# The last step of blockwise triangular inverses as products of quarters, in a two-layer hybrid decoder trunk

## The chip, the cores and the metric

The kernel runs on one NeuronCore of a Trainium2 chip. The metric is device time in microseconds (us) from start to end of one execution, as a median over several runs. In the profile, PE is TensorE (PEld its weight loads), DVE is VectorE, ACT is ScalarE, POOL is GpSimd, and SP is SyncE, whose queue issues most DMAs.

## What is computed

One inference step of a decoder trunk with two layers, for 512 prompt positions and for 8 samples of 4 positions. In each layer an input projection feeds four mixers (RWKV-7, S5, gated delta, windowed attention), whose outputs are joined, projected and followed by an MLP. The change concerns RWKV-7 and gated delta alone. The gated delta mixer works on chunks of 64 positions and solves one lower triangular system for each chunk and head:

```python
def step(S, inp):
    qc, kc, vc, bc, gc = inp
    ...
    A = jnp.where(strict, bc[..., :, None] * decay * jnp.einsum('bhtd,bhjd->bhtj', kc, kc), 0.0)
    gam = jnp.exp(G)[..., None]
    rhs = bc[..., None] * (vc - gam * jnp.einsum('bhvk,bhtk->bhtv', S, kc))
    U = lax.linalg.triangular_solve(eye + A, rhs, left_side=True, lower=True, unit_diagonal=True)
    ...
```

RWKV-7 is a recurrence over single positions in the reference. The kernel puts it into the same form with chunks of 64. For both mixers the kernel computes the inverses of the unit triangular matrices themselves, 64x64 each, and multiplies with them.

## The kernel before

The prompt is cut in two halves of 256 columns, and the second half also carries the 32 sample columns. For each layer and half the kernel runs an input projection, the mixers, an output projection and an MLP. The projections and MLPs are the dense work: weights arrive by DMA as 128x512 parts (`wraw`), ScalarE casts each part to a high part `whi` (three buffers), VectorE subtracts to get the rest `wlo`, and TensorE makes 12 matmuls from each part (`dense`, `load_part`). The mixers of one half are interleaved with the dense work of another. The framework orders the instructions on each engine when the program is built, from modelled times and from the priorities in `PRIO`; on the chip each engine then runs its own list in that order.

A half has 4 chunks and 4 heads for each of the two mixers, so 16 triangular matrices of 64x64. They lie in a tile of 128 partitions x 8 x 64: chunks in the upper and the lower 64 partitions, 8 matrices side by side in each. `tri_begin` inverts the diagonal blocks of 16 on VectorE. `tri_end` then doubles the block size twice, from 16 to 32 and from 32 to 64. It holds `lt` (the strict triangle, transposed), `t16` (the inverse so far) and `t16t` (its transpose), and `work`. Its helper `mm` makes 16 matmuls with 64 rows, 64 columns of weights and 64 moving columns, two for each of the 8 places, on the two diagonal quarters of TensorE's array. The first doubling makes `lt * t16`, masks it (constant `blk16`, which is -1 in the blocks that are wanted and 0 elsewhere), and makes two products that are added to `t16` and `t16t`. The second doubling, the step that is changed, makes `lt * t16`, masks it with `blk32`, makes one more product with `t16t`, and adds it to `t16t`.

`rw_stage3` and `gd_stage3` call `tri_end`, and hand its result to `inv_apply`, which multiplies it with keys and values. With two layers, two halves and two mixers there are 8 calls. All matmuls are recorded under L220 (`mm` of the class), all `tt` operations on VectorE under L236, `acopy` under L232 (without scale) and L233 (with one). In the trace `t16`, `t16t`, `work` and RWKV's `lt` appear as `t`, and gated delta's `lt` as `g`.

Of the kernel before, what the change touches and what calls it, by code (L numbers as in the profile page):

```python
# [12 lines left out]
ALU = mybir.AluOpType  # L13
# [126 lines left out]
class K:  # L140
# [180 lines left out]
    def tri_end(self, lt, t16, t16t, work):  # L321
        def mm(a, b):

            out = self.ps([128, 8, 64])
            for hb in range(8):
                for c in range(2):
                    cs = slice(64 * c, 64 * c + 64)
                    self.mm(out[cs, hb], a[cs, hb], b[cs, hb])
            return out

        bm = lambda n: self.c(n).unsqueeze(1).to_broadcast([128, 8, 64])

        self.tt(work, mm(lt, t16), bm("blk16"))
        a, b = mm(t16t, work), mm(work, t16t)
        self.tt(t16, a, t16, ALU.add)
        self.tt(t16t, b, t16t, ALU.add)
        self.tt(work, mm(lt, t16), bm("blk32"))
        self.tt(t16t, mm(work, t16t), t16t, ALU.add)
        return t16t


# [1719 lines left out]
```

## Time and profile before

| | |
|---|---|
| median of 3 runs | 1626.77 us (1626.5 to 1631.62) |
| the profiled execution, whole | 1630.86 us |
| its span, first to last instruction | 1629.1 us |
| TensorE busy | 1555.1 us, 95% |
| VectorE busy | 1195.3 us, 73% |
| ScalarE busy | 961.8 us, 59% |
| GpSimd busy | 318.0 us, 20% |
| mean granted TensorE clock | 0.984 |

An fp32 matmul appears as two instructions, each with a weight load and a matmul. Durations of single matmuls overlap, since they are pipelined; the time that a group really takes is read from its starts. The busy time of a group is the union of its instructions' times.

### The profile page before, as it was taken

How to read it: one execution, taken by the hardware profiler on the slowest of the kernel's cores; microseconds unless marked ns; L12 is line 12 of the kernel's file. 1: busy time of each engine (PE TensorE's matmuls, PEld its weight loads, DVE VectorE, ACT ScalarE, POOL GpSimd, SP SyncE). 2: the span in 40 equal slices, each digit the busy share in tenths (PEclk: the TensorE clock that was granted, in tenths of full speed). 3: DMA queues.
4: the chain of work that ended last, by engine and by line, in shares of the span. 5: the costliest groups of instructions: out<-in, count | busy, mean ns of one | idle time of the engine just before them, and what ended most of it. 6: DMA issues, size and time to landing. Idle time of an engine off the chain costs nothing. (4 is left out here: it accounts for less than half of the span.)

```text
span 1629.1 us, 38773 instructions
## 1 busy us (share of the span) xinstructions
PE 1555.1 (95%) x14528; PEld 1453.4 (89%) x14528; DVE 1195.3 (73%) x2843; ACT 961.8 (59%) x2086; POOL 318.0 (20%) x618
## 2 busy tenths in 40 slices
PE   7989989899999999899999999999999999999996
PEld 7978978689889999888989999989888889999996
DVE  6898786976876867787595567879679755856665
ACT  6766648643455567765454467886444556755544
POOL 4751251000310428100020002620013001200001
PEclk9999999999999999999999999999999999999998
DMA  7645444443566565535365555535436655655552
GB/s 232 200 114 136 143 134 148 109 130 114 173 211 201 171 204 204 182 112 139 105 217 173 167 161 197 180 109 151 138 121 208 205 193 185 210 189 166 163 170 101
DMA packets 203112, 267.38 MB, mean 164 GB/s; under 512 B 81114, under 2 KB 95772, under 8 KB 202508
## 3 DMA queue, kind: packets, MB, share of 16 engines
q1 hardware_dynamic: 199180, 249.94, 48.9%
q0 software_dynamic: 3744, 14.96, 2.5%
q8 instruction: 114, 1.87, 0.5%
q14 instruction: 74, 0.61, 0.1%
HBM read 237.95 MB, written 28.58 MB: 164 GB/s over the span
## 5 line engine op out<-in xcount | busy, mean ns | idle before, releaser
L232 ACT CAST whi<-wraw 128x512 fp32r<-128x512 f32 x752 | 462.6, 619 | 419.2 <-PE ps L220 264.7
L236 DVE TENSOR_TENSOR wlo<-wraw,whi 128x512 fp32r<-128x512 f32 x752 | 534.9, 716 | 209.2 <-ACT whi L232 188.0
L220 PE MATMUL ps<-h,whi 128*128 128x288 f32 (+1 forms) x3264 | 519.5, 297 | 8.4 <-ACT h L228 4.4
L220 PEld LDWEIGHTS ps<-h,whi 128*128 128x128 f32 x3264 | 451.3, 191 | 25.8 <-ACT h L228 6.0
L220 PE MATMUL ps<-f,whi 128*128 128x288 f32 (+1 forms) x2752 | 421.9, 292 | 5.9 <-ACT whi L232 5.8
L220 PEld LDWEIGHTS ps<-f,whi 128*128 128x128 f32 x2752 | 372.0, 189 | 17.1 <-ACT whi L232 7.4
L220 PE MATMUL ps<-h,wlo 128*128 128x288 f32 (+1 forms) x1632 | 285.9, 295 | 5.4 <-DVE wlo L236 5.1
L220 PEld LDWEIGHTS ps<-h,wlo 128*128 128x128 f32 x1632 | 235.8, 191 | 12.3 <-DVE wlo L236 7.8
L220 PE MATMUL ps<-f,wlo 128*128 128x288 f32 (+1 forms) x1376 | 235.8, 292 | 1.7 <-DVE wlo L236 1.7
L220 PEld LDWEIGHTS ps<-f,wlo 128*128 128x128 f32 x1376 | 195.9, 189 | 5.3 <-DVE wlo L236 2.9
L236 POOL TENSOR_TENSOR sums<-sums,d 128x288 f32<-128x288 f32 (+1 forms) x54 | 51.2, 948 | 519.0 <-ACT d L228 517.7
L220 PE MATMUL ps<-r,r 64*64 64x64 f32 (+7 forms) x1184 | 67.8, 236 | 12.7 <-POOL r L236 3.8
L236 DVE TENSOR_TENSOR acc<-acc,ps 128x256 f32<-128x256 f32 (+1 forms) x96 | 41.7, 435 | 49.8 <-PE ps L220 49.7
L220 PEld LDWEIGHTS ps<-r,r 64*64 64x64 f32 (+4 forms) x1184 | 55.9, 140 | 23.2 <-issue 5.9
L232 ACT CAST f<-d 128x288 fp32r<-128x288 f32 (+1 forms) x128 | 53.3, 417 | 35.3 <-DVE d L236 35.3
L228 ACT ACTIVATE d<-ps 128x288 f32<-128x288 f32 (+1 forms) x152 | 59.8, 393 | 8.1 <-PE ps L220 6.1
L236 DVE TENSOR_TENSOR f<-d,f 128x288 fp32r<-128x288 f32 (+1 forms) x128 | 56.7, 443 | 7.4 <-ACT f L232 7.4
L236 DVE TENSOR_TENSOR d<-d 128x288 f32<-128x288 f32 (+1 forms) x128 | 56.7, 443 | 0.0
L228 ACT ACT_TABLE_LOAD x43 | 55.2, 1283 | 0.8
L220 PEld LDWEIGHTS ps<-t,t 64*64 64x64 f32 x1024 | 32.5, 135 | 4.7 <-issue 1.1
L220 PE MATMUL ps<-t,t 64*64 64x64 f32 x1024 | 36.3, 220 | 0.3 <-DMA t<-diag 0.2
L232 ACT COPY r<-ps 64x128 f32<-64x128 f32 (+2 forms) x56 | 20.4, 369 | 26.4 <-PE ps L625 11.6
(404 smaller groups left out, 1851.6 us busy)
## 6 DMA issues: line engine op xcount, KB each, us to landing
wraw<-in_w_up SPq DMA_DIRECT2D x256, 256.0 KB, 2.8
wraw<-in_w_down SPq DMA_DIRECT2D x256, 256.0 KB, 2.9
wraw<-in_w_in SPq DMA_DIRECT2D x176, 256.0 KB, 3.0
wraw<-in_w_out SPq DMA_DIRECT2D x64, 256.0 KB, 3.2
t<-diag SPq DMA_DIRECT2D x32, 128.0 KB, 3.2
x<-acc POOLq DMA_DIRECT2D x3, 1152.0 KB, 6.8
x<-acc POOLq DMA_DIRECT2D x3, 1024.0 KB, 6.4
xs<-mix SPq DMA_DIRECT2D x8, 288.0 KB, 2.9
```

The costliest lines, as they stand in the source:

```text
L220: return self.nc.tensor.matmul(out=out, lhsT=lhsT, rhs=rhs, start=start, stop=stop)
L228: return self.nc.scalar.activation(out=out, in_=in_, func=func, scale=scale, bias=bias, **kw)
L232: return self.nc.scalar.copy(out, in_)
L236: return (eng or self.nc.vector).tensor_tensor(out=out, in0=a, in1=b, op=op)
```

## The change

The second doubling no longer multiplies whole 64x64 blocks. Only the quarter that is wanted is computed: a product of 32x32 blocks, 16 of them for each product as before, with 32 rows, 32 columns of weights and 32 moving columns. The tile positions in the array change with it: rows 0 and 64 with columns 32 and 96 in the first product, rows 32 and 96 with columns 0 and 64 in the second. The mask with `blk32` on VectorE is gone. In its place ScalarE copies the first product from PSUM into `work` with the scale -1, in two operations on 32 partitions x 256 elements. The last addition on VectorE, before one operation on 128 partitions x 512 elements, becomes two on 32 partitions x 256 elements, which write only the quarter that changes.

```diff
         a, b = mm(t16t, work), mm(work, t16t)
         self.tt(t16, a, t16, ALU.add)
         self.tt(t16t, b, t16t, ALU.add)
-        self.tt(work, mm(lt, t16), bm("blk32"))
-        self.tt(t16t, mm(work, t16t), t16t, ALU.add)
+
+        def quarter(a, b, o):
+            out = self.ps([128, 8, 64])
+            for hb in range(8):
+                for c in (0, 64):
+                    k = slice(c + 32 - o, c + 64 - o)
+                    m = slice(o, o + 32)
+                    n = slice(32 - o, 64 - o)
+                    self.mm(out[c + o:c + o + 32, hb, 0:32], a[k, hb, m], b[k, hb, n])
+            return out[:, :, 0:32]
+
+        p = quarter(lt, t16, 32)
+        for c in (32, 96):
+            self.acopy(work[c:c + 32, :, 0:32], p[c:c + 32], scale=-1.0)
+        p = quarter(work, t16t, 0)
+        for c in (0, 64):
+            t = t16t[c:c + 32, :, 32:64]
+            self.tt(t, p[c:c + 32], t, ALU.add)
         return t16t
```

## Rows read from the trace of the kernel before

**Rows 1.** The page, part 1: busy us of each engine (share) xinstructions.
```profile
PE 1555.1 (95%) x14528; PEld 1453.4 (89%) x14528; DVE 1195.3 (73%) x2843; ACT 961.8 (59%) x2086; POOL 318.0 (20%) x618
```
**Rows 2.** Windows: length, then PE, PEld, DVE, ACT, POOL busy (instructions), PEclk, DMA.
```profile
133.00:190.00 57.00, 56.88 (x834) 51.54 (x833) 42.58 (x126) 32.45 (x95) 12.52 (x42) 1.00 0.50 150
327.00:377.00 50.00, 49.84 (x736) 44.16 (x735) 35.15 (x93) 23.92 (x59) 0.00 (x0) 1.00 0.44 124
745.00:795.00 50.00, 50.00 (x722) 44.80 (x721) 31.91 (x84) 21.68 (x53) 0.25 (x2) 1.00 0.40 118
1146.00:1189.00 43.00, 43.00 (x693) 38.75 (x691) 27.47 (x73) 18.63 (x46) 0.00 (x0) 1.00 0.41 120
sum 200.00, PE 199.72 PEld 179.25 DVE 137.10 ACT 96.69 POOL 12.77; mean PE 49.93 PEld 44.81 DVE 34.28 ACT 24.17 POOL 3.19
```
**Rows 3.** The chain that ended last, pieces: start us, us, what.
```profile
1167.60 27.17 PE ps L220 x446
```
**Rows 4.** Timeline of VectorE and TensorE: start us, us, instructions (merged).
```profile
147.96 0.67 DVE L236 TENSOR_TENSOR t<-ps,cst 128x512 f32<-128x512 f32 x1
149.97 1.15 PE L220 MATMUL ps<-t,t 64*64 64x64 f32 x32
```
**Rows 5.** Timeline of TensorE, 177 to 184 us.
```profile
177.32 1.15 PE L220 MATMUL ps<-t,t 64*64 64x64 f32 x32
178.40 0.45 PE L220 MATMUL ps<-r,r 128*64 128x64 f32 x8
...
183.04 0.27 PE L220 MATMUL ps<-rwS,r 64*64 64x64 f32 x1
...
183.26 0.44 PE L220 MATMUL ps<-rwS,r 64*64 64x64 f32 x5
```
**Rows 6.** Windows as in rows 2; the counts include matmuls still in flight.
```profile
154.90:154.96 0.06, 0.06 (x10) 0.06 (x9) 0.06 (x1) 0.00 (x0) 0.00 (x0) 1.00 0.89 205
154.90:155.08 0.18, 0.18 (x19) 0.18 (x16) 0.18 (x2) 0.00 (x0) 0.00 (x0) 1.00 0.86 196
141.80:141.90 0.10, 0.10 (x5) 0.10 (x6) 0.10 (x1) 0.04 (x1) 0.10 (x1) 1.00 0.96 328
141.80:143.07 1.27, 1.27 (x45) 1.27 (x46) 1.20 (x3) 0.04 (x1) 0.42 (x1) 1.00 0.51 152
```
**Rows 7.** Groups by form (rows*columns loaded, moving): xcount, busy us, mean ns, idle before.
```profile
L220 PE MATMUL ps<-t,t 64*64 64x64 f32 x1024 | 36.3, 220 | 0.3 <-DMA t<-diag 0.2
L220 PE MATMUL ps<-cv 64*64 64x128 f32 x96 | 5.1, 282 | 0.4 <-DVE g L236 0.4
L220 PE MATMUL ps<-c,s 64*64 64x8 f32 x128 | 4.6, 199 | 0.0
L220 PEld LDWEIGHTS ps<-t,t 64*64 64x64 f32 x1024 | 32.5, 135 | 4.7 <-issue 1.1 <-DMA t<-diag 1.0 <-DVE swst L236 0.2
L220 PEld LDWEIGHTS ps<-r,r 64*128 64x128 f32 x128 | 11.7, 187 | 4.2 <-DVE r L236 2.4 <-issue 1.0 <-DVE wlo L236 0.2
L220 PEld LDWEIGHTS ps<-cst,c 16*32 16x32 f32 x4 | 0.3, 102 | 0.0
```
**Rows 8.** VectorE groups by form; then L233 on ScalarE: ns min/median/max.
```profile
L236 DVE TENSOR_TENSOR t<-ps,t 128x512 f32<-128x512 f32 x24 | 16.4, 684 | 7.1 <-PE ps L220 7.1
L236 DVE TENSOR_TENSOR c<-ps,cst 32x256 f32<-32x256 f32 x16 | 5.6, 403 | 0.0
L233 ACT ACTIVATE g<-ps x8: 362/384/384, 160.1 to 1167.6; 128x256 f32<-128x256 f32 x8
```
**Rows 9.** Waits of ScalarE: who for whom, us in total, times, longest.
```profile
ACT whi L232 <- PE ps L220: 264.7, 285, 5.4
```
**Rows 10.** Timeline of ScalarE and TensorE near 234.4 us; a window after it.
```profile
238.61 0.63 ACT L228 ACTIVATE r<-r 128x512 f32<-128x512 f32 x1 [4.06 <-DVE r L245]
239.58 1.33 PE L220 MATMUL ps<-e,cst 128*128 128x288 f32 x2 [5.15 <-ACT e L232]
236.10:242.90 6.80, 3.32 (x12) 3.03 (x13) 4.13 (x11) 2.86 (x5) 5.84 (x18) 0.50 0.16 56
```

## The prediction

> **What bounds the kernel now.** I read the profile from the whole to the place of the change. The busy shares come first: TensorE is busy 95% of the span, VectorE 73%, ScalarE 59% [rows 1]. An average hides stages, so next come the busy times of the four stretches in which the eight inverses end (two in each, one for RWKV and one for gated delta): in 200 us TensorE is busy 199.72 us, VectorE 137.10, ScalarE 96.69, and the granted clock is 1.00 in all four [rows 2]. The chain of waits says the same from the other side: in these stretches it runs along TensorE itself, in the last of them for 27.17 us in one piece [rows 3]. So in these places the end is set by how long TensorE needs for its queue; a VectorE or ScalarE operation there costs nothing as long as its result is there before TensorE reaches the product that reads it.
>
> How much room that leaves: the mask step of the last 32-to-64 stage of one call starts at 147.96 us and takes 0.67 us; TensorE begins the product that reads it at 149.97 us, 1.34 us after its end [rows 4]. Of the sixteen VectorE results of this stage (eight masks, eight additions) this one has the least room. Dense matmuls fill the time between.
>
> **What one product costs.** A product is sixteen 64x64x64 matmuls, which stand in the trace as 32 instructions (fp32 is run as two). One such product starts at 177.32 us and the next work at 178.40 us: 1.08 us [rows 5]. In the steady state forty starts lie in the 1.17 us from 141.90 to 143.07 us (45 counted against 5), 29.3 ns each [rows 6]. Two diagonal quarters of the array work side by side, so one quarter takes about 58 ns for an instruction, and 32 x 29.3 = 0.94 us; the other 0.14 us is the first load and the change of tile shape.
>
> What sets these 58 ns? The form with 8 moving columns instead of 64 has 4.6 us for 128 instructions, 36 ns each, and the one with 64 columns 36.3 us for 1024, 35 ns [rows 7]. So fewer moving columns alone buy nothing. But that form still loads 64 columns of weights. Weight loads last 102 ns for 32 columns, 135 for 64, 187 for 128 [rows 7]: 0.8 to 1.0 ns a column, and 64 columns make some 53 ns. Matmuls go from 220 to 282 ns for 64 more moving columns [rows 7], 1.0 ns a column. Load and stream each need about 53 ns of the 58 and overlap; the rest, about 5 ns, is overhead. The change halves both sides, the loaded and the moving columns. I therefore take 27 + 5 = 32 ns for one quarter and 16 ns for an instruction with two quarters side by side.
>
> **The change, part by part.**
> *Products.* Sixteen products (two in each of eight calls) keep their 32 instructions and go from 29.3 to about 16 ns: 512 x 13.3 ns = 6.8 us less TensorE time. Bounds: nothing, if something other than the columns sets the pace; and 29.3 - 13 = 16 ns, 8.3 us, if the closest packing that the trace shows is reached: nine starts in 0.12 us, 13 ns each, where two groups of 64x64 matmuls overlap (19 counted against 10) [rows 6]. I take 6.8, nearest to the rows on columns, and hold the rate for possible because of that burst. No change of tile shape is added: a product stood between dense 128x128 work before and still does.
>
> *VectorE.* Removed: eight masks and eight additions over 128x512, 0.684 us each by the row of the additions, whose shape the masks have too [rows 8], 10.9 us. Added: sixteen additions over 32x256, 0.403 us by the row of that form [rows 8], 6.4 us. VectorE has 4.5 us less, hidden either way: it is idle for 63 of the 200 us [rows 2].
>
> *ScalarE.* Added: sixteen copies of 32x256 from PSUM with a constant scale; the nearest row, the same kind over 128x256, has 0.384 us [rows 8]: 6.1 us, hidden by the 103 us in which ScalarE is idle there. Thirty-two partitions could take half of it, and the stride in PSUM could double it, 3 to 12 us in all; either is far below that cover. If the cover were gone, all 6.1 us would stand on the path.
>
> *The chain of one call.* Before: product 1.08, mask 0.68, product 1.08, addition 0.68, 3.52 us. After: 0.65, two copies 0.77, 0.65, two additions 0.81, 2.88 us, where 0.65 is 32 x 16 ns and the same 0.14. It gets shorter, so the later reader has, if anything, more room than the 1.34 us above. The new wait is on ScalarE's queue: the copy waits there for its product, and behind it stand the casts of the dense weights, for which TensorE waits in turn. But those casts run ahead: ScalarE spends 264.7 us of the whole run waiting for TensorE to free a cast buffer [rows 9]. No DMA is moved, and SyncE's and GpSimd's queues get nothing new.
>
> **The sum.** The profiled execution took 1630.86 us, 1.8 us more than its span; 1630.86 - 6.8 = 1624.1 us. It lies 4.1 us above the median of the three runs, 1626.77 us, and the measured time will be a median: 1626.8 - 6.8 = 1620.0. I give 0.5 us back for the ends of the stretches, where TensorE waits on other engines: **1620.5 us**. What is late next after a stretch are waits on chains of GpSimd, VectorE and ScalarE; a stretch that ends 0.9 to 1.7 us earlier could lengthen them, but they hang on TensorE's products and move with it.
>
> **The rivals.** *First, the columns do not set the pace.* For it speaks that 8 and 64 moving columns go at the same 36 and 35 ns [rows 7]. If a floor on an instruction stands at the 24 ns that nine starts in the 0.22 us from 183.04 to 183.26 us show [rows 5], the gain is 512 x 5.3 ns = 2.7 us, 1624.1; if the pace is all floor, 1626.8. I put this rival at 1625. Against it speaks the burst of 13 ns. The Trainium skill, "TensorE: Matmul & The Clock Gate", section "Wait — 56ns, not 53.3ns?", states such a floor: start to start never below about 25 ns however few columns. By that figure, an estimate, the gain would be 512 x 4.3 = 2.2 us. This trace disagrees for instructions in different quarters, which start 13 ns apart, and cannot say whether it holds within one quarter of 32x32, where my 32 ns lies above it anyway.
>
> *Second, slower: ScalarE's queue holds TensorE up.* The order of instructions on each engine is fixed at build from modelled times, so new operations on two queues redraw it from the first inverse (133 us) to the end. The place where this costs is visible before: at 234.4 us TensorE stands still for 5.15 us because ScalarE's copy of a dense product is queued behind an S5 activation that itself waits 4.06 us for VectorE [rows 10]; and a stretch of 6.8 us at a granted clock of 0.50 (1.2 GHz) follows [rows 10], which costs up to 3.4 us more. One such event is 8.5 us. The sixteen copies wait in the same queue. The rival decides from the point where a copy waits longer than the 1.34 us and the casts ahead allow; 0.9 us of standstill in each of the eight calls eats the gain. Two new events of the full price give 1620 + 17 = 1637. Against it: in the four stretches before, TensorE lost only 0.28 us in all, with 46 to 95 ScalarE operations in each [rows 2].
>
> *Third, the redraw goes the other way* and removes that one event: 1620 - 8.5 = 1611.5. *Fourth, the gain is taken back in part* by the waits behind the stretches: 1624.
>
> **How the numbers follow.** About 0.3% (4.9 us) is what a measurement of this kernel can tell from no change. Forecast, 1617 to 1621.8: 0.45, counted as faster. Third rival, 1608 to 1616: 0.07, faster. First rival, 1623 to 1627: 0.19, same. Fourth, 1622 to 1626: 0.09, same. Slower rival, 1632 to 1642: 0.20. That makes 0.52 faster, 0.28 same, 0.20 slower. The forecast's own range is 1617 to 1622; to leave out no more than 2 in 10, the range reaches to 1612 below and to 1635 above, into the near half of the slower rival.
>
> **What would show it.** The 32x32 products in the profile of the changed kernel: 32 instructions from start to next start in about 0.65 us, 16 ns apart in the steady state, shows the first step right; 0.8 us or more, the first rival. Weight loads of 32x32 at about 102 ns show the halved load. ScalarE copies near 0.38 us and VectorE additions near 0.40 us, with TensorE busy throughout the four stretches, show the cover. TensorE's idle total and the stretches of granted clock 0.50 tell the second and third rival. The prediction is wrong if TensorE waits for the copies, or if its waits elsewhere move by more than the 6.8 us.

## The result and the profile after

The changed kernel takes 1641.11 us (median of 11 runs, 1636.13 to 1647.87), the kernel before 1631.62 us beside it (11 runs, 1626.50 to 1637.62). The ratio is 1.0062, 95% interval 1.0041 to 1.0083: 0.6% slower, clear of the noise, where 1620.5 us and 0.4% faster were forecast, and outside the range. The profiled execution took 1645.58 us with a span of 1643.8 us.

The local steps came out as worked out. First the page, part 1, of the changed kernel (to be held against rows 1):

```profile
PE 1568.3 (95%) x14528; PEld 1460.8 (89%) x14528; DVE 1195.3 (73%) x2843; ACT 966.7 (59%) x2102; POOL 316.2 (19%) x618
```

The windows of the four stretches in which its inverses end (rows 2; length, then PE, PEld, DVE, ACT, POOL busy, PEclk, DMA):

```profile
134.50:188.00 53.50, 53.36 (x754) 48.27 (x754) 41.38 (x121) 34.17 (x100) 12.79 (x44) 1.00 0.51 149
339.00:388.00 49.00, 49.00 (x712) 43.21 (x712) 33.46 (x89) 24.73 (x62) 0.00 (x0) 1.00 0.39 112
758.00:808.00 50.00, 50.00 (x746) 44.06 (x745) 30.47 (x82) 23.08 (x57) 0.65 (x2) 1.00 0.38 115
1157.00:1199.00 42.00, 42.00 (x682) 37.44 (x681) 25.47 (x66) 19.48 (x49) 0.00 (x0) 1.00 0.40 117
sum 194.50, PE 194.36 PEld 172.98 DVE 130.77 ACT 101.45 POOL 13.45; mean PE 48.59 PEld 43.24 DVE 32.69 ACT 25.36 POOL 3.36
```

The timeline of the first call's last step (rows 4 and 5), with lines in between left out:

```profile
146.04 0.69 PE L220 MATMUL ps<-t,t 32*32 32x32 f32 x32
...
146.66 1.34 PE L220 MATMUL ps<-h,whi 128*128 128x288 f32 x8
146.78 0.78 ACT L233 ACTIVATE t<-ps 32x256 f32<-32x256 f32 x2 [3.74 <-PE ps L220]
...
149.92 0.69 PE L220 MATMUL ps<-t,t 32*32 32x32 f32 x32
...
150.88 0.86 DVE L236 TENSOR_TENSOR t<-ps,t 32x256 f32<-32x256 f32 x2
```

And the groups by form (rows 7 and 8):

```profile
L220 PE MATMUL ps<-t,t 32*32 32x32 f32 x384 | 9.3, 193 | 0.0
L220 PEld LDWEIGHTS ps<-t,t 32*32 32x32 f32 x384 | 7.5, 107 | 2.3 <-issue 0.7 <-ACT xs L228 0.2
L236 DVE TENSOR_TENSOR t<-ps,t 32x256 f32<-32x256 f32 x16 | 6.6, 416 | 5.4 <-PE ps L220 5.1
L233 ACT ACTIVATE t<-ps 32x256 f32<-32x256 f32 x16 | 6.0, 376 | 5.7 <-PE ps L220 5.0 <-issue 0.2
```

A product of quarters takes 0.62 us from its first start (146.04) to the next work (146.66), where 1.08 us stood before. The copies end at 147.56 us, 2.36 us before TensorE reads them; in all eight calls they are done at least 1.9 us ahead. In the four stretches TensorE is busy for 194.36 of 194.50 us at the full clock, as before. So nothing at the place of the change explains a slower kernel.

The profiled spans do. Here is the mean granted clock, the changed kernel's first and the one of the kernel before under it:

```profile
core 0: 1643.8 us, clock 0.975
```

```profile
core 0: 1629.1 us, clock 0.984
```

At two levels, 1.00 and 0.50, that is 2 x 0.025 x 1643.8 = 82 us at half clock, against 2 x 0.016 x 1629.1 = 52 us; and the 30 us more of half clock are 15 us. By the pages TensorE is without work for 75.5 us of the span (1643.8 - 1568.3) against 74.0, so hardly any of the loss is a new wait. Where much of the additional half clock lies, four pairs of windows of the changed kernel show, each with the stretch ahead of a fall and the one behind it:

```profile
387.20:394.80 7.60, 7.60 (x187) 6.71 (x185) 3.54 (x21) 1.17 (x2) 1.07 (x2) 1.00 0.35 115
394.80:401.60 6.80, 6.80 (x29) 4.83 (x27) 3.01 (x13) 0.99 (x2) 0.00 (x0) 0.50 0.00 1
1238.10:1241.30 3.20, 3.20 (x59) 3.07 (x58) 2.01 (x6) 1.31 (x3) 0.50 (x2) 0.99 0.22 82
1241.30:1248.10 6.80, 6.80 (x45) 5.21 (x43) 2.88 (x8) 0.99 (x3) 0.37 (x2) 0.50 0.01 2
299.60:306.00 6.40, 3.75 (x37) 3.14 (x36) 6.30 (x23) 3.43 (x9) 0.00 (x0) 1.00 0.19 53
306.00:312.80 6.80, 4.39 (x27) 3.33 (x28) 6.45 (x13) 3.15 (x7) 0.59 (x1) 0.50 0.17 31
251.40:258.20 6.80, 4.96 (x28) 4.01 (x26) 4.47 (x11) 5.52 (x15) 0.00 (x0) 1.00 0.39 123
258.20:265.00 6.80, 6.34 (x26) 5.62 (x27) 2.37 (x8) 2.17 (x6) 0.00 (x0) 0.50 0.37 120
```

The first two pairs are the surprise: TensorE is busy for the whole of 7.60 us and of 3.20 us, and then the clock stands at 0.50 for 6.80 us. What it was busy with, its timeline in the changed kernel tells:

```profile
386.70 0.64 PE L220 MATMUL ps<-f,whi 128*128 128x256 f32 x4
387.27 1.15 PE L220 MATMUL ps<-g,t 64*64 64x64 f32 x32
...
393.65 1.22 PE L220 MATMUL ps<-c,s 64*64 64x8 f32 x35
394.80 2.07 PE L220 MATMUL ps<-r,cst 128*128 128x512 f32 x2
396.80 0.47 PE L220 MATMUL ps<-gdS,g 64*64 64x64 f32 x2
397.20 0.79 PE L220 MATMUL ps<-f,whi 128*128 128x256 f32 x2
```

Between the dense matmuls (`whi`, `wlo`) at 386.70 and at 397.20 us lie about 10 us; up to 394.80 us there are only matmuls on 64x64 and 128x64 parts of the array. The kernel before has work of the same kind there, and its dense matmuls come back after 5.6 us, at 387.6 us:

```profile
382.00:387.60 5.60, 5.60 (x154) 5.13 (x152) 3.15 (x20) 0.98 (x2) 1.07 (x2) 1.00 0.56 202
387.60:394.40 6.80, 6.80 (x56) 5.76 (x57) 5.21 (x24) 2.50 (x5) 0.00 (x0) 1.00 0.15 45
```

The second pair is of the same kind. In the changed kernel two groups that use little of the array stand back to back:

```profile
1238.19 1.97 PE L220 MATMUL ps<-cst,gdlb 32*128 32x32 f32 x16
1240.08 1.99 PE L220 MATMUL ps<-cv,s 64*64 64x8 f32 x50
```

In the kernel before their starts are 7.4 us apart, with dense matmuls between:

```profile
1223.45 1.97 PE L220 MATMUL ps<-cst,gdlb 32*128 32x32 f32 x16
...
1227.95 1.10 PE L220 MATMUL ps<-h,whi 128*128 128x256 f32 x8
...
1230.89 2.04 PE L220 MATMUL ps<-cv,s 64*64 64x8 f32 x64
```

The Trainium skill, "TensorE: Matmul & The Clock Gate", section "HAM oscillation — how this bites in real kernels", puts such falls down to gaps in which TensorE is idle. By that rule alone the falls at 394.8 and 1241.3 us would not be there; here the trace disagrees. It agrees for the third pair, where TensorE stands still for 3.33 us, waiting for VectorE:

```profile
308.06 0.44 PE L224 MATMUL ps<-cst,xs 128*128 128x128 f32 x1 [3.33 <-DVE r L236]
```

Ahead of the fourth fall TensorE is without work for 1.84 of 6.80 us, and 1.35 of them it waits for a cast of weights that stands behind other work in ScalarE's queue:

```profile
257.40 0.51 PE L220 MATMUL ps<-h,whi 128*128 128x256 f32 x2 [1.35 <-ACT whi L232]
```

That these two waits bring on the falls behind them was not tried; it needs another order on VectorE and ScalarE too.

None of these places holds an instruction that the change touches. But the framework drew the order anew at build: from the first inverse on, 3797 of the 11906 places in TensorE's list hold another instruction than before, 973 of 2809 in VectorE's, 469 of 2009 in ScalarE's and 139 of 997 in SyncE's, which issues the DMAs. So there were two theories to tell apart: *order* (the new list costs, the new work gains) and *work* (the quarters or the copies cost).

### The profile page after: what moved, and what is told of

It is laid out like the page before. It is cut to its first block, busy times and chain, and to the rows that moved or that the text cites. A ratio compares the mean times of both kernels' runs of the same rounds, so it can differ in the third digit from the quotient of the medians.

```text
span 1643.8 us, 38794 instructions
## 1 busy us (share of the span) xinstructions
PE 1568.3 (95%) x14528; PEld 1460.8 (89%) x14528; DVE 1195.3 (73%) x2843; ACT 966.7 (59%) x2102; POOL 316.2 (19%) x618
## 5 line engine op out<-in xcount | busy, mean ns | idle before, releaser
L220 PE MATMUL ps<-h,whi 128*128 128x288 f32 (+1 forms) x3264 | 524.8, 299 | 12.5 <-ACT h L228 5.9
L220 PEld LDWEIGHTS ps<-h,whi 128*128 128x128 f32 x3264 | 455.9, 193 | 31.2 <-ACT h L228 7.1
L220 PEld LDWEIGHTS ps<-h,wlo 128*128 128x128 f32 x1632 | 237.4, 192 | 13.5 <-DVE wlo L236 8.0
L220 PEld LDWEIGHTS ps<-t,t 64*64 64x64 f32 (+1 forms) x1024 | 27.8, 124 | 6.3 <-DMA t<-diag 2.0
L220 PE MATMUL ps<-t,t 64*64 64x64 f32 (+1 forms) x1024 | 31.8, 210 | 1.6 <-DMA t<-diag 1.5
```

The lines of the kernel that those rows point to most:

```text
L220: return self.nc.tensor.matmul(out=out, lhsT=lhsT, rhs=rhs, start=start, stop=stop)
```

## The experiments

**One word on the sums.** For each kernel the time lost to the clock is taken as (1 - mean granted clock) x span, averaged over its runs, and the rest is its mean time less that. A half-clock stretch in which TensorE idles anyway is counted too, and the rest scatters by some 3 us from run to run, so differences of it are good to 1 or 2 us at best. Within one kernel a us more of this loss went with only 0.56 us more time from run to run (199 runs), so the column says too much rather than too little; a count that doesn't rest on it stands behind e12. The changes of tile are counted in the trace: how often a TensorE matmul has another size of tile than the one before.

| kernel (runs) | ratio to before | mean us | lost to the clock | rest | changes of tile |
|---|---|---|---|---|---|
| before (23) | 1 | 1632.4 | 28.0 | 1604.3 | 536 |
| changed (11) | 1.0062 [1.0041, 1.0083] | 1642.1 | 38.8 | 1603.3 | 574 |
| e1 new work, old order (12) | 0.9972 [0.9958, 0.9986] | 1627.6 | 29.9 | 1597.6 | 540 |
| e2 old work, new order (6) | 1.0107 [1.0087, 1.0126] | 1649.7 | 37.9 | 1611.8 | 574 |
| e3 old work, redraw a (12) | 1.0013 [0.9998, 1.0028] | 1634.3 | 27.8 | 1606.5 | 544 |
| e4 old work, redraw b (6) | 1.0064 [1.0041, 1.0087] | 1642.7 | 33.1 | 1609.6 | 535 |
| e5 new order behind 615 us (12) | 1.0012 [0.9998, 1.0025] | 1634.5 | 32.0 | 1602.5 | 568 |
| e6 new order ahead of it (12) | 1.0019 [0.9999, 1.0038] | 1635.6 | 35.4 | 1600.2 | 546 |
| e7 quarters, no copies (12) | 0.9967 [0.9953, 0.9982] | 1626.7 | 29.3 | 1597.5 | 540 |
| e8 copies, whole products (12) | 1.0011 [0.9995, 1.0027] | 1633.7 | 29.4 | 1604.3 | 536 |
| e9 groups of 4 moved ahead (6) | 1.0092 [1.0071, 1.0113] | 1647.3 | 40.6 | 1606.7 | 590 |
| e10 more changes of tile (6) | 1.0073 [1.0052, 1.0095] | 1643.1 | 30.4 | 1612.8 | 637 |
| e11 fewer changes of tile (6) | 0.9891 [0.9870, 0.9912] | 1613.8 | 27.1 | 1586.6 | 476 |
| e12 whole blocks moved ahead (6) | 1.0046 [1.0030, 1.0062] | 1640.3 | 32.2 | 1608.0 | 574 |

Runs of the kernel before stand beside every group of these; their medians lie between 1631.6 and 1633.2 us, their rests between 1603.2 and 1605.0.

### Work and order taken apart (e1, e2)

The order is held by edges between neighbours of a wanted list, engine by engine, which make no wait on the chip. `ORDER` is a list of emission numbers; for e1 it is the order of the kernel before with the changed kernel's instructions in it (the sixteen copies are left free), for e2 the changed kernel's with the old instructions.

```diff
 def build(tc, ins, outs):
     with ExitStack() as ctx:
         K(tc, ctx, ins, outs).body()
+    made, last = list(tc.nc.cur_bb.bb.instructions), {}
+    for i in ORDER:
+        e = str(made[i].engine)
+        if e in last:
+            tc.add_manual_dep(made[i], last[e], K.NOSYNC, reason="order")
+        last[e] = made[i].name
```

> The changed kernel's instructions, held on every engine in the order of the kernel before (the sixteen ScalarE copies, which have no counterpart there, are free to be placed). Theory 'order': the changed kernel lost because its queues were redrawn at build, not through its own operations; then this one shows the gain of the forecast, about 6.8 us or 0.4% less than the kernel before run beside it (ratio 0.994 to 0.998), with granted-clock stretches of 0.50 as few as before (some 40 us in all ahead of the tail). Rival 'work': the 32x32 products or the copies themselves cost the time (clock, waits); then it is as slow as the changed kernel, ratio 1.004 to 1.008.

> The kernel before, held on every engine in the order of the changed kernel (its eight masks are free to be placed). Theory 'order': slower than the changed kernel by the 6.8 us that the quarters save, so a ratio to the kernel before of 1.008 to 1.013, with some 70 us at a granted clock of 0.50. Rival 'work': as fast as the kernel before, 0.998 to 1.002.

The new work in the old order is faster than both kernels, 0.9972; the old work in the new order is slower than both, 1.0107. So the new work gains 0.28% in the old order and 1.0062/1.0107, 0.45%, in the new one, and the order costs 0.9 to 1.1%. The rest of e1 is 6.7 us below that of the kernel before, close to the forecast's 6.8 us; its time lost to the clock is 8.9 us below the changed kernel's. Theory *work* is out. Since e1, e7 and e8 hold the same old order and e8, with products of whole blocks, comes out like the kernel before (below), the holding itself costs nothing that these runs show.

### Another redraw with the work unchanged (e3, e4)

```diff
-PRIO = {..., 'rwt': 300, ..., 'gdt': 200}
+PRIO = {..., 'rwt': 290, ..., 'gdt': 200}   (e3)
+PRIO = {..., 'rwt': 300, ..., 'gdt': 300}   (e4)
```

> The kernel before with one priority changed (rwt 300 to 290): the same instructions, of which 1130 of TensorE's 11906 stand elsewhere in its queue. Theory 'order': the time moves by 0.2 to 0.8% to either side with no change of work. Rival 'work': within 0.2% of the kernel before.

> The kernel before with another priority changed (gdt 200 to 300): the same instructions, of which 3286 of TensorE's 11906 stand elsewhere, about as many as in the changed kernel (3797). Theory 'order': the time moves by 0.3 to 1% to either side. Rival 'work': within 0.2% of the kernel before.

A priority that changes no instruction moves 1130 places of TensorE's list in e3 and 3286 in e4, and the time by +0.1% and +0.6%; e3 stays under the 0.2% expected, and its interval holds 1. So a redraw as large as the one that came with the change can be worth as much as the whole measured difference, and more than the edit's 6.8 us. By the mean clock e4 loses 5.1 us more to the clock and has 5.3 us more rest, without more changes of tile; what that rest is wasn't settled.

### The two halves of the edit (e7, e8)

```diff
-            self.acopy(work[c:c + 32, :, 0:32], p[c:c + 32], scale=-1.0)
+            w = self.c("blk32")[c:c + 32, 0:32].unsqueeze(1).to_broadcast([32, 8, 32])
+            self.tt(work[c:c + 32, :, 0:32], p[c:c + 32], w)                      (e7)
```

```diff
-        p = quarter(lt, t16, 32)
+        p = mm(lt, t16)
-            self.acopy(work[c:c + 32, :, 0:32], p[c:c + 32], scale=-1.0)
+            self.acopy(work[c:c + 32, :, 0:32], p[c:c + 32, :, 0:32], scale=-1.0)
-        p = quarter(work, t16t, 0)
+        p = mm(work, t16t)                                                        (e8)
```

> Half of the change: products of quarters as in the changed kernel, but the sign by VectorE (two multiplications of 32x256 with the constant that is -1) in place of ScalarE's two copies; all engines held in the order of the kernel before. Theory 'products': the 6.8 us come from TensorE's instructions alone and ScalarE's copies cost and bring nothing, so this is like the whole change in the old order: ratio 0.9972 (0.9955 to 0.9990). Rival 'copies': the gain in the old order comes from the shorter way over ScalarE; then about 1.0000.

> The other half: products of whole 64x64 blocks as in the kernel before, but their wanted quarter is copied with the sign by ScalarE (two copies of 32x256) and added in two halves by VectorE; all engines held in the order of the kernel before. Theory 'products': TensorE has all its columns again, ratio 1.0000 (0.9985 to 1.0015). Rival 'copies': 0.9972.

The products of quarters alone bring the whole gain, 0.9967; the copies and the halved additions alone bring and cost nothing, 1.0011 with 1 inside the interval. Which engine takes the sign makes no difference that these runs show.

### Where the order costs (e5, e6)

The edit is that of e1 with a mixed list: at about 615 us both lists hold the same instructions again on all engines.

> The changed kernel's instructions, all five engines held in the order of the kernel before up to the place (615 us in the profile of the changed kernel) where both lists hold the same instructions again, and in the changed kernel's order behind it. Theory 'places': the redrawn order costs where it makes long runs of small matmuls; behind 615 us these are the runs from 1204.9 and from 1238.0 us, with stretches of granted clock 0.50 at 1210.5 and 1241.3 us. In the profiled executions the changed kernel is 10.8 us behind the one with the old order (615.8 against 605.0 us at the same dense part) at the cut and 21.9 us at the end, so about half of the cost lies behind: of the 14.7 us between the two ratios (1.0062 and 0.9972) about 7, and the ratio here is 1.0015 (1.0000 to 1.0030), with half-clock stretches near 1200 and 1230 us and none of 6.8 us from 380 to 400. Rival 'whole': the time depends on the redraw as a whole and can't be put down to places; then this kernel may come out anywhere from 0.997 to 1.006 and its half-clock stretches don't come back at the two places.

> The reverse: the changed kernel's order on all five engines up to the same place, the order of the kernel before behind it. Theory 'places': the long runs of small matmuls from 299 and from 387 us are there, and half-clock stretches of 6.8 us each at their ends; the cost is the other half, 7 to 8 us over the old order, ratio 1.0020 (1.0005 to 1.0035); and the parts add up: (this - 0.9972) + (the kernel with the new order behind - 0.9972) = 0.0090 within 0.003. Rival 'whole': the parts don't add up, and the stretches lie elsewhere.

0.0040 over e1 for the part behind, 0.0047 for the part ahead, 0.0087 together; the whole is 0.0090. So the cost splits into two parts that add up, within their intervals. Of the half-clock stretches that were expected, e5 has the one near 1230 us (6.8 us at 1232.3) and none near 1200; e6 has both (6.8 us at 309.0, 10.2 us at 394.3).

### The price of a change of tile (e10, e11)

e5 and e6 left a question: in both halves the rest had grown too. The new order has 34 changes of tile more than e1. In e10 four dense matmuls are moved into the middle of a group of small ones in 49 places; in e11 short groups of dense matmuls are moved ahead of the small group before them in 35 places. Both start from e1, and only TensorE's list is edited:

```diff
-  small x16 | dense x12
+  small x8 | dense x4 | small x8 | dense x8          (e10)
-  dense | small a | dense x4 | small b
+  dense, dense x4 | small a, small b                 (e11)
```

> The whole change, held in the order of the kernel before, but in 49 places four of the dense matmuls that follow a group of small ones are moved ahead into the middle of that group; nothing is left out. TensorE changes its tile shape some 97 times more (540 times in the trace with the old order, 574 in the changed kernel's). Theory 'changes': each costs 0.14 us, the part of a product's 1.08 us that its 32 starts don't explain; 97 x 0.14 = 13.6 us, ratio 1.0055 (0.10 to 0.20 us a change: 1.003 to 1.009), with idle time and half-clock stretches near those of the old order (56 and 41 us). So the 34 more changes of the redrawn order are 5 us of its cost, the rest its half-clock stretches. Rival 'clock alone': changes of tile cost nothing, dense matmuls in between rather keep the clock up: 0.997 or below.

> The reverse: the whole change, held in the order of the kernel before, but in 35 places a short group of dense matmuls between two groups of small ones is moved ahead of the first, so that both join their like; joined groups of small ones stay under 2 us. Some 64 changes of tile shape less. Theory 'changes': 64 x 0.14 = 9 us less than with the old order alone, ratio 0.992 (0.990 to 0.995), if TensorE doesn't wait for the delayed chains instead. Rival 'clock alone': 0.997, or above it where the joined groups let the clock fall.

97 changes more raise the rest by 15.2 us, 0.16 us each; 64 fewer lower it by 11.0 us, 0.17 us each, and bring e11 a little below the 0.990 expected. TensorE is shown as busy all the while, as the first part of the page shows, for e1, e10 and e11 in turn:

```profile
PE 1549.3 (96%) x14528; PEld 1446.1 (89%) x14528; DVE 1194.4 (74%) x2843; ACT 969.4 (60%) x2102; POOL 320.8 (20%) x618
```

```profile
PE 1571.9 (96%) x14528; PEld 1460.5 (89%) x14528; DVE 1192.1 (73%) x2843; ACT 968.5 (59%) x2102; POOL 317.4 (19%) x618
```

```profile
PE 1539.8 (95%) x14528; PEld 1445.7 (90%) x14528; DVE 1192.8 (74%) x2843; ACT 967.9 (60%) x2102; POOL 320.7 (20%) x618
```

The same 14528 instructions stand as 1549.3, 1571.9 and 1539.8 us of busy time. The Trainium skill, "TensorEngine Tiling (Array Packing)", section "Key Properties", says that a change of the tiling mode drains TensorE; the runs fit that and show a price, though no trace shows the draining itself.

The starts in e1's trace show the price directly, where TensorE doesn't wait and the clock is 1.00. From a dense matmul to a small one they lie 0.222 us apart (mean of 175), and 0.130 us from a dense one to the next; from a small one to a dense one 0.166 us (179), and 0.040 us from a small one to the next of its size. There and back costs 0.092 + 0.126 = 0.218 us, so 0.11 us a change. That is 10.7 of the 15.2 us and 7.0 of the 11.0; where the other 4 us or so of each lie is open. It is the tile and not the type of number, which changes with it in e10 and e11: from a dense matmul to an fp32 one on the same 128x128 tile the starts lie 0.139 us apart, and on the way back only 0.031 us, where fp32 ones follow each other after 0.197 us.

So the 34 changes more of the new order cost 3.7 us by the starts and up to 5.8 us by the prices of e10 and e11; the rests of the changed kernel and e1 differ by 5.7. e4 and e12 warn against taking this as an exact sum: their rests are some 5 us higher without any more changes. e11 is also the version that beats both kernels: 1613.75 us against 1633.1, 1.1% less.

### The granted clock (e9, e12)

Both keep the changed kernel's order and move dense matmuls ahead on TensorE alone: e9 in groups of four at four places, e12 in whole blocks at three.

```diff
-  small (from 387 us, 10 us) | dense x24 ...
+  small | dense x12 | small | dense x12 | small | dense ...     (e12; 12 from 1205 us)
-  gdlb x8 | cv,s x25 | ... | dense x24
+  gdlb x8 | dense x24 | cv,s x25 | ...                          (e12; from 1238 us)
```

> The changed kernel's own order on all engines, but in four places (the runs of small matmuls from 317, 387, 1205 and 1238 us) TensorE gets 8 to 12 of the dense matmuls that follow, in groups of 4 spread over the run; nothing else is moved and no work is left out. Theory 'clock': it is the run of small matmuls that lets the granted clock fall although TensorE is busy; the stretches of 0.50 at 323.1 (3.4 us), 394.8 (6.8), 1210.5 (3.4) and 1241.3 (6.8) go, 20.4 us at half clock, 10.2 us; ten more groups of dense matmuls are some 20 more changes of tile shape at about 0.1 us (the dense group of four at 386.70 us is followed after 0.57 us by the next work, against 4 x 0.117 = 0.47), 2 us; so 8 us less than the changed kernel, ratio 1.0013 (0.9995 to 1.0030). Rival 'work': the clock of a run doesn't depend on what fills it, or the stretches only move by some us; half-clock total ahead of the tail stays near 71.7 us, and the ratio is 1.0062 or, with the changes of tile shape, up to 1.0075.

> The changed kernel's own order, but in three places whole blocks of the dense matmuls that follow are moved ahead on TensorE: two blocks of 12 into the run from 387 us, 12 into the run from 1205 us, and 24 between the two sparse groups (16 instructions of 32*128 32x32 and 50 of 64*64 64x8) that stand back to back from 1238 us and were 7 us apart in the kernel before. Unlike the earlier run with groups of four this doesn't add changes of tile shape (none more by the count of the lists). Theory 'clock': the half-clock stretches at 394.8 (6.8 us), 1210.5 (3.4) and 1241.3 us (6.8) go, 17 us at half clock, 8.5 us; time lost to the clock, by the mean granted clock of all runs, falls from 38.8 to about 30 us, ratio 1.0010 (0.9995 to 1.0030). Rival 'elsewhere': the falls come at other places instead or stay, lost time stays at 38 us or more and the ratio at 1.0062 (1.0045 to 1.0080). If TensorE waits for weights that aren't cast yet, its idle time rises over 59.2 us and the ratio with it.

e9 came out against its theory, 1.0092. In its trace the stretches at 394.8 and 1210.5 us are gone, but the one at 323.1 us is there (at 325.2 us), and at 1240.0 us one of 10.2 us stands where the two sparse groups were only parted by four dense matmuls; there are 16 more changes of tile, 2.6 us at 0.16 us each; and over its six runs the loss to the clock, 40.6 us, isn't lower than the changed kernel's 38.8. That run alone would have refuted the theory. e12 removes all three stretches, as its windows show:

```profile
387.40:394.40 7.00, 7.00 (x126) 6.03 (x125) 1.63 (x7) 0.59 (x1) 1.07 (x2) 1.00 0.37 125
394.40:401.60 7.20, 6.75 (x111) 5.62 (x110) 4.21 (x26) 2.00 (x5) 0.00 (x0) 1.00 0.01 2
1233.40:1240.00 6.60, 6.60 (x93) 6.35 (x91) 1.98 (x5) 1.67 (x4) 0.50 (x2) 1.00 0.11 40
1240.00:1246.80 6.80, 5.40 (x63) 3.85 (x62) 4.90 (x16) 1.88 (x5) 0.37 (x2) 1.00 0.25 86
1205.00:1212.00 7.00, 7.00 (x118) 5.69 (x117) 4.71 (x27) 2.01 (x4) 0.00 (x0) 1.00 0.11 39
```

The clock stays at 1.00 in all five, and the loss to the clock falls by 6.6 us to 32.2, over six runs. So it is how small and dense matmuls follow each other that lets the clock fall at these places, though TensorE is busy. What that is worth in time the ratios don't show: 1.0046 lies above the 1.0010 expected, inside the rival's range, and its interval overlaps with the changed kernel's; the mean is only 1.9 us lower, since the rest is 4.7 us higher. In the trace TensorE does wait where the dense matmuls that were moved ahead are missing, here for VectorE:

```profile
1245.13 0.72 PE L220 MATMUL ps<-r,r 64*64 64x72 f32 x16 [1.40 <-DVE r L245]
```

Over its whole span, however, TensorE is without work no longer than in the changed kernel, 74.1 us against 75.5, and this execution's rest is no higher: 1638.48 us is 7.1 us less than the changed kernel's profiled execution, 6.7 of them by the mean clock. So these waits don't explain the higher mean rest, which stays open.

A count in the traces does without mean clock and rest: for every matmul that starts at half clock, the time to the next start, less idle time, against what the same two kinds of matmul take at full clock in all the traces. For the changed kernel it gives 30.1 us where the mean clock gives 41.1, for e1 16.6 where it gives 26.0. It and the 0.11 us for a change of tile account for most of what the order costs in two pairs of profiled executions:

| profiled executions | apart | half clock | idle time | changes of tile | left over |
|---|---|---|---|---|---|
| changed and e1 (new work) | 21.9 us | 13.5 | 3.0 | 34, 3.7 | 1.7 |
| e2 and before (old work) | 20.6 us | 12.6 | 2.1 | 38, 4.2 | 1.7 |

## Why the prediction was wrong, step by step

*TensorE bounds the stretches* (rows 1 to 3): right, 194.36 of 194.50 us. One of its two readings carried less than it was given: the chain of rows 3 can be followed back to 1014 us only, so it spoke for the last of the four stretches, and the other three rested on the busy times.

*The products, 6.8 us.* Right in size and cause. 0.62 us stand against the forecast 0.65, 0.46 us less than before in each of sixteen products, 7.4 us; weight loads take 107 ns against 102, and the rest of e1 is 6.7 us lower, that of e7 7.6 us against the runs beside it. The first rival, a floor of 24 ns from start to start, falls: 32 starts of a product lie within 0.50 us, in pairs with 7 ns inside a pair and 25 ns to the next, 16 ns on average. Whether a floor of about that size holds within one quarter stays open, since the trace doesn't tell which start belongs to which quarter.

*VectorE and ScalarE* (rows 8, 9): right where it mattered. The copies take 376 ns (0.384 us was taken), the additions 416 (0.403 us), VectorE's total stays at 1195.3 us where 4.5 us less were worked out, and ScalarE's casts still run ahead of TensorE:

```profile
ACT whi L232 <- PE ps L220: 268.7, 296, 6.5
```

e8 shows that both together cost nothing.

*The order around the change* is the step that failed. The forecast took the surroundings as given, with the redraw at nothing in its sum, and let it appear only in rivals: one that slows, with one mechanism, ScalarE's queue, at 0.20, and one that removes an event of the same kind, at 0.07. Little of that mechanism came. The event near 234 us (rows 10) is there in the changed kernel too, with a shorter standstill:

```profile
239.38 0.63 ACT L228 ACTIVATE r<-r 128x512 f32<-128x512 f32 x1 [3.15 <-issue]
...
241.39 1.33 PE L220 MATMUL ps<-e,cst 128*128 128x288 f32 x2 [3.92 <-ACT e L232]
```

One new event of its kind is the wait of 1.35 us before 257.40 us with 6.8 us at half clock behind it, up to 4.8 us where the rival took 17. It stands in the five kernels with the new order in front (changed, e2, e6, e9, e12) and in none with the old order there. So it is in the main luck that 1641.11 us lies within this rival's 1632 to 1642.

What happened has two terms that the prediction's sum didn't list, and idle time is the least of it. First, the new list lets the clock fall more often, and not only behind a standstill, as the rival had it: 8.9 us between the changed kernel and e1 by the mean clock, 13.5 us by the count in the profiled executions. Three falls under full load go with three edits of TensorE's list (e12). Second, it changes tile 34 times more, 3.7 us by the starts and at most 5.8. The two mean times differ by 14.5 us; that the order makes this difference is shown by e1 and e2, its split by measurements that agree to a few us. Against it stand the 6.7 us of the products.

The prediction's sentence that no change of tile shape is added was wrong in both places. Held in the old order, the products of quarters add four changes (540 in e1 and e7 against 536 before and in e8), since four products are followed by other 64x64 matmuls and not by dense ones; and the list added 34. It had a price at hand: it set 0.14 us aside for the load and the change of tile in each product. That no DMA is moved holds for the edit alone, too: the list of SyncE changed in 139 places.

*What would show it.* The stretches of granted clock 0.50 were named as a sign and told the truth; TensorE's idle total, 75.5 against 74.0 us, was named beside them and would have said that nothing had happened. Of the two signs of being wrong that it named, neither came: no copy is late, and the waits moved by 1.5 us in sum.

*The base.* The sum was set on the median of three runs, 1626.77 us; the median of eleven is 1631.62. That is 4.9 us of the 20.6 us by which the forecast missed; as ratios, 0.9962 was forecast, 1.0062 came, and 0.9972 would have come in the old order.

## What to carry to other kernels

Where a framework draws the order at build, an edit of a few instructions changes the whole list behind it, and that alone was worth about 1% here: measure the edit with the old order held and a redraw without the edit before either is believed. On a busy TensorE read two things that busy time hides: the granted clock behind long runs of small matmuls, and how often the tile size changes. Grouping small matmuls with small ones (up to about 2 us) and dense with dense gained more than the edit.

## What the runs showed of the hardware

The granted clock fell to 0.50 (1.2 GHz) for 6.8 us after 7.60 us in which TensorE was busy all the time, with 64x64 and 128x64 matmuls only, and after 3.20 us of 32x128 tiles and of 8-column matmuls; with dense matmuls put between, 24 in each place, it stayed at 1.00. It is not certain at every such place: the kernel before kept 1.00 behind its 5.6 us of small matmuls from 382.0 us, and e1, with the same order, fell there for 3.4 us:

```profile
386.00:389.40 3.40, 3.40 (x12) 2.06 (x10) 1.15 (x6) 0.62 (x1) 0.00 (x0) 0.50 0.00 0
```

A change of tile size costs 0.11 us by the starts, and 0.16 to 0.17 us in the time of e10 and e11, shown as busy time; a change from dense matmuls to fp32 ones on the same tile and back costs nothing by the starts. The 32 instructions of a product of 32x32 fp32 matmuls on two quarters start 16 ns apart on average, those of 64x64 ones 30 ns.
